# First-norm and indexer-key roots as a GpSimd power with one Newton step, and the first layer's indexer products with the low part last

## The chip, the cores and the metric

The kernel runs on one core of one Trainium2 chip. The metric is the device time of one execution in microseconds. The time given for a kernel is the median of several runs. A profile is one further execution, recorded by the hardware profiler.

The core has five engines, each with its own in-order instruction queue: PE (TensorE, matrix products; its weight loads are listed as PEld), DVE (VectorE), ACT (ScalarE), POOL (GpSimd) and SP (SyncE, which here only issues DMAs). [...]

## The reference

Two decoder layers on one sequence of 512 tokens of width 1024. What matters here is the beginning of the program and of each layer:

```python
x = layer_norm(x, ln_in_g, ln_in_b)                 # the first norm, over 1024 columns
for i in range(2):
    h = x @ w_in[i]                                 # columns partitioned: ..., qi (256), ki (32), wi (8)
    ki = rope(layer_norm(ki, idx_k_g, idx_k_b))     # the indexer key: a norm over 32 columns
    qi = rope(qi)
    # indexer: scores of qi with ki, weighted by wi, pick 128 keys for each query (top_k)
    # then sliding-window attention, sparse attention over the picked keys, output projection,
    # x = LN(alpha*x + mix); gated FFN and per-layer embedding; x = LN(...)
```

`layer_norm(x) = (x - mean) * rsqrt(var + 1e-5) * g + b`. Both changes concern the `rsqrt` of the first norm and of the indexer key's norm, and the product of the normed x with the 296 indexer columns (qi, ki, wi) in the first layer.

## The kernel before, in words

The 512 tokens are four blocks of 128 (`t` = 0 to 3). Every matrix product is made of three passes (`mm3`, lines 323 to 327): each operand is split into a high part (rounded to the fast float format) and a low part (the remainder), and the products high x high, high x low of the weight, and low of x x high are summed in one bank. x in transposed form lies in `fh` (high) and `fl` (low).

How a block gets from memory to its indexer product:

- **The norm** (`ln_in`, lines 386 to 400). Block 0 has its mean and variance from DVE. Blocks 1 to 3 have theirs from ACT (`ln_in_sums`, lines 380 to 384: a sum, a small multiply, and `squares` at line 377). DVE then subtracts the mean and multiplies with g in two halves (line 397), `rstd_of` (lines 352 to 365) makes the root, and line 400 multiplies with the root and adds b, again in two halves. Gains and biases are read from four banks filled by PE at the start (line 345).
- **The root**, `rstd_of(var, n)`: one DVE instruction for -0.5(var + eps) (line 357), one that makes a first guess by arithmetic on the bits (line 358), then three Newton steps of two DVE instructions for each of n columns (lines 363 and 364). That is 8 DVE instructions for n = 1 and 14 for n = 2.
- **To features** (`to_features`, lines 432 to 441): PE transposes the block in two groups of four (line 438), ACT copies each group to `fh` (line 440), DVE subtracts to get `fl` (line 441).
- **The indexer product** (`project`, lines 535 to 546, called from `start` at line 826): eight rows `k` of the weights, three matmuls of 296 columns each, 24 for a block, in the order high, weight-low, x-low for each `k`.
- **After it** (`gi_out`, lines 555 to 594): DVE takes mean and variance of the 32 key columns (lines 562 to 564); for each pair of blocks the key's root is made (line 578, n = 2: blocks 0 and 1 when block 1 is done, 2 and 3 when block 3 is done); `rope` (lines 502 to 517) multiplies with the rotary tables on DVE (line 511), adds on POOL (line 513), copies the high part (line 516) and subtracts the low part on POOL (line 517). PE's transposes of the results follow later (line 523), then the indexer's scores (lines 638 to 651: PE 645, ACT 647, DVE 648), then top-k on DVE (lines 659 and 660).

Beside this run the weights: SP loads them in pieces (line 240), ACT rounds the high part (line 278), POOL subtracts the low part (line 279); five split pieces fit (`W_AHEAD`). A piece's place is given back by `w_rel` when the last product with it has been written down; for the indexer weights that is in block 3. And the rotary tables (`rotary`, lines 453 to 491): products on ACT (line 473), 6 and then 4 additions of 128 x 192 on POOL (line 477), two sines on ACT, some copies.

What sets the order: the Python code writes the instructions down in an order in which streams (`start`, `index`, `rest`, `attention`, `topk`) are interleaved by estimated costs, and the planner of the tile framework then arranges each engine's queue from its own timing estimates, an earlier-written instruction first among those that it takes to be ready. On the chip each queue runs strictly in the order arranged. `tc.issue_after(ins)` adds one more rule: what is written inside it comes behind `ins` on the same engine. All of `gi_out(t)` for t < 3 of the first layer is put behind the norm of block t + 1 in this way (line 822).

## Time and profile before

| | |
|---|---|
| median of 3 runs | 1251.45 us (1251.43 to 1251.7) |
| the profiled execution's own time | 1251.81 us |
| its span (first to last recorded instruction) | 1249.7 us |
| PE busy | 1225.9 us, 98% |
| DVE, POOL, ACT busy | 765.2, 682.9, 576.4 us |
| POOL weight splits of line 279 | 148, 351.3 us |

A row of the timeline begins with the start in us from the beginning of the span and the duration in us; then come engine, line of the kernel, operation, what is written and read, the shape, and how many consecutive instructions are merged in the row. In square brackets stands how long the engine had been idle before, and whose end released it. A row of the windows gives, for a stretch of time, its length and then the busy time of PE, PEld, DVE, ACT and POOL. A row of the waits gives who waited for whom: us in total, how often, the longest.

### The profile page before, as it was taken

How to read it: one execution, taken by the hardware profiler on the slowest of the kernel's cores; microseconds unless marked ns; L12 is line 12 of the kernel's file. 1: busy time of each engine (PE TensorE's matmuls, PEld its weight loads, DVE VectorE, ACT ScalarE, POOL GpSimd, SP SyncE). 2: the span in 40 equal slices, each digit the busy share in tenths (PEclk: the TensorE clock that was granted, in tenths of full speed). 3: DMA queues.
4: the chain of work that ended last, by engine and by line, in shares of the span. 5: the costliest groups of instructions: out<-in, count | busy, mean ns of one | idle time of the engine just before them, and what ended most of it. 6: DMA issues, size and time to landing. Idle time of an engine off the chain costs nothing.

```text
span 1249.7 us, 18006 instructions
## 1 busy us (share of the span) xinstructions
PE 1225.9 (98%) x6552; PEld 1029.9 (82%) x6552; DVE 765.2 (61%) x1678; ACT 576.4 (46%) x1193; POOL 682.9 (55%) x555
## 2 busy tenths in 40 slices
PE   7999999999999999999999999999999999999996
PEld 5998777988888888888899987689888888888885
DVE  7699954682727272726677998286555555555365
ACT  6577763442434343433337787534343333333331
POOL 6885532566566666663169754234757575757400
PEclk9999999999999999999999999999999999999999
DMA  5232311333232323034033203114323333321321
GB/s 177 78 92 85 95 42 35 119 118 118 85 118 84 118 85 118 18 118 140 2 89 114 101 21 117 52 54 149 99 87 105 97 105 99 103 83 52 101 84 50
DMA packets 89264, 112.74 MB, mean 90 GB/s; under 512 B 5460, under 2 KB 66132, under 8 KB 89176
## 3 DMA queue, kind: packets, MB, share of 16 engines
q1 hardware_dynamic: 88504, 111.58, 28.5%
q8 instruction: 51, 0.84, 0.3%
q14 instruction: 37, 0.30, 0.1%
q10 hardware_dynamic: 672, 0.03, 0.0%
HBM read 109.49 MB, written 2.10 MB: 89 GB/s over the span
## 4 chain that ended last, share of the span: by engine, by line
PE 82%; POOL 5%; DVE 3%; issue 3%; ACT 3%; DMA 3%; SPq 0%; DVEq 0%; ACTq 0%; POOLq 0%
PE bank L325 24%; PE bank L326 24%; PE bank L327 24%; PE bank L715 3%; PE bank L684 3%; PE bank L721 2%; POOL wsp L279 2%; DMA wst<-in_w_pg_dram 2%; POOL wsp L257 1%; PE bank L523 1%; PE bank L438 1%; PE bank L732 1%; ACT wsp L278 1%; DVE slot L273 1%; POOL slot L517 1%
## 5 line engine op out<-in xcount | busy, mean ns | idle before, releaser
L279 POOL TENSOR_TENSOR wsp<-wst,wsp 128x1024 fp32r<-128x1024 f32 (+2 forms) x148 | 351.3, 2389 | 244.4 <-ACT wsp L278 240.8
L326 PE MATMUL bank<-fl,wsp 128*128 128x512 f32 (+1 forms) x768 | 284.8, 372 | 0.4 <-DVE fl L441 0.4
L325 PE MATMUL bank<-fh,wsp 128*128 128x512 f32 (+1 forms) x768 | 283.6, 372 | 1.0 <-ACT fh L440 1.0
L327 PE MATMUL bank<-fh,wsp 128*128 128x512 f32 (+1 forms) x768 | 283.1, 371 | 0.0
L278 ACT CAST wsp<-wst 128x1024 fp32r<-128x1024 f32 (+2 forms) x148 | 151.6, 1033 | 166.4 <-PE bank L327 126.2
L325 PE MATMUL bank<-wsp,fh 128*128 128x256 f32 (+3 forms) x512 | 165.2, 326 | 3.6 <-DVE work L648 2.0
L874 DVE TENSOR_TENSOR t2k<-bank,t2k 128x512 f32<-128x512 f32 x44 | 30.4, 692 | 222.0 <-PE bank L327 222.0
L326 PEld LDWEIGHTS bank<-fl,wsp 128*128 128x128 f32 x768 | 144.6, 188 | 25.7 <-DVE fl L441 0.9
L325 PEld LDWEIGHTS bank<-fh,wsp 128*128 128x128 f32 x768 | 143.6, 188 | 26.8 <-ACT fh L440 1.9
L327 PEld LDWEIGHTS bank<-fh,wsp 128*128 128x128 f32 x768 | 144.6, 188 | 24.9
L327 PE MATMUL bank<-wsp,fl 128*128 128x256 f32 (+3 forms) x512 | 163.7, 322 | 1.4 <-DVE fl L441 0.8
L326 PE MATMUL bank<-wsp,fh 128*128 128x256 f32 (+3 forms) x512 | 164.7, 322 | 0.0
L257 POOL TENSOR_TENSOR wsp<-slot,wsp 128x512 fp32r<-128x512 f32 x100 | 141.6, 1442 | 29.0 <-ACT wsp L256 29.0
L325 PE MATMUL bank<-wsp,slot 128*128 128x512 f32 x392 | 153.8, 392 | 0.0
L326 PE MATMUL bank<-wsp,slot 128*128 128x512 f32 x392 | 152.7, 390 | 0.0
L327 PE MATMUL bank<-wsp,slot 128*128 128x512 f32 x392 | 148.4, 390 | 0.0
L790 DVE TENSOR_TENSOR x<-bank,x 128x512 f32<-128x512 f32 x140 | 91.5, 684 | 88.5 <-PE bank L327 88.5
L904 ACT CAST slot<-t2k 128x256 fp32r<-128x256 f32 (+1 forms) x104 | 49.8, 497 | 144.1 <-DVE t2k L874 102.5
L257 POOL TENSOR_TENSOR wsp<-t2k,wsp 128x512 fp32r<-128x512 f32 x40 | 57.5, 1448 | 92.4 <-ACT wsp L256 92.4
L325 PEld LDWEIGHTS bank<-wsp,fh 128*128 128x128 f32 x512 | 97.6, 191 | 11.9 <-ACT fh L440 2.4
L327 PEld LDWEIGHTS bank<-wsp,fl 128*128 128x128 f32 x512 | 97.5, 191 | 7.9 <-DVE fl L441 1.1
L326 PEld LDWEIGHTS bank<-wsp,fh 128*128 128x128 f32 x512 | 98.0, 191 | 6.5 <-issue 1.2
(152 smaller groups left out, 2004.6 us busy)
## 6 DMA issues: line engine op xcount, KB each, us to landing
wst<-in_w_gu_dram SPq DMA_DIRECT2D x88, 512.0 KB, 3.5
slot<-in_w_down_dram SPq DMA_DIRECT2D x80, 256.0 KB, 2.8
wst<-in_w_in_dram SPq DMA_DIRECT2D x16, 512.0 KB, 3.6
wst<-in_w_o_dram SPq DMA_DIRECT2D x16, 512.0 KB, 3.8
wst<-in_w_pg_dram SPq DMA_DIRECT2D x16, 512.0 KB, 4.2
wst<-in_w_in_dram SPq DMA_DIRECT2D x8, 256.0 KB, 2.7
lng<-in_ln_g_dram SPq DMA_DIRECT2D x4, 512.0 KB, 4.8
lnb<-in_ln_b_dram SPq DMA_DIRECT2D x4, 512.0 KB, 5.5
```

Source lines behind the costliest of these rows:

```text
L257: G.tensor_tensor(w[:, 1, j], src[j], w[:, 0, j], OP.subtract)
L278: A.copy(w[:, 0, :a * n], st[:, :a * n])
L279: G.tensor_tensor(w[:, 1, :a * n], st[:, :a * n], w[:, 0, :a * n], OP.subtract)
L325: PE.matmul(o, sh, mh, start=start, stop=False, skip_group_check=again)
L326: PE.matmul(o, sh, ml, start=False, stop=False, skip_group_check=again)
L327: PE.matmul(o, sl, mh, start=False, stop=stop, skip_group_check=again)
L684: PE.matmul(ps[:, o:o + nn], qT[kind, t, g][:, j * 128:(j + 1) * 128], kT[c, s][:, k0:k0 + nn], start=(s == 0), stop=(s == 1))
L715: PE.matmul(o[u * 64:(u + 1) * 64], vt[b0 + b][:, c * 64:(c + 1) * 64], pts[b][:, u], start=b == 0, stop=b == nb - 1)
L721: PE.transpose(ps[:, j * 128:(j + 1) * 128], es[j][:, b * 128:(b + 1) * 128], idf)
L790: V.tensor_tensor(xt[t][:, c], ps, xt[t][:, c], OP.add)
L874: V.tensor_tensor(a, ps[1, f], a, OP.mult)
L904: A.copy(h[0], src)
```

## The change

Three edits. First, a new function `root_of` takes the place of `rstd_of` in `ln_in` (four uses, n = 1) and in the indexer key's norm of `gi_out` (two uses in each layer, n = 2). The other norms keep `rstd_of`. `root_of` has one DVE instruction for the variance plus eps, one POOL instruction (`tensor_tensor` with the operation `pow`, against a constant tile of -0.5), and three DVE instructions that make one Newton step. In the n = 1 form the first of these three overwrites what the power reads, so it has to come after it. Second, the first six of the ten additions on POOL for the rotary tables are put behind block 0's power. Third, in the first layer `project_fresh` writes the indexer product of a block with the 16 matmuls on the high part of x first and the 8 on the low part last; the places of the weight pieces are given back among the last eight matmuls of block 3.

```diff
+    half = small.tile([128, 2], F32, name="half", tag="half", bufs=1)
+    G.memset(half, -0.5)
+
+    def root_of(var, n=1, of=1):
+        v = sm(n, f"lnv{n}")
+        s = sm(n, f"lns{n}")
+        t = sm(n, f"lnt{n}")
+        V.tensor_scalar(v, var, of * EPS, 1.0 / of, op0=OP.add, op1=OP.mult)
+        last["root"] = G.tensor_tensor(s, v, half[:, :n], OP.pow).ins
+        if n == 1:
+            V.tensor_scalar(v, v, -0.5, None, op0=OP.mult)
+            V.tensor_scalar(t, s, s, v, op0=OP.mult, op1=OP.mult)
+            V.tensor_scalar(s, t, 1.5, s, op0=OP.add, op1=OP.mult)
+        else:
+            V.tensor_tensor(t, s, s, OP.mult)
+            V.scalar_tensor_tensor(t, t, -0.5, v, op0=OP.mult, op1=OP.mult)
+            V.scalar_tensor_tensor(s, t, 1.5, s, op0=OP.add, op1=OP.mult)
+        return s
...
-        rs = rstd_of(var, of=of)                    # in ln_in
+        rs = root_of(var, of=of)
...
-            for pr in products:                     # in rotary
-                G.tensor_tensor(ang[:, :n], pr, ang[:, :n], OP.add)
+            with tc.issue_after(last["root"]) if bits == 7 else nullcontext():
+                for pr in products:
+                    G.tensor_tensor(ang[:, :n], pr, ang[:, :n], OP.add)
...
+    def project_fresh(ws, n, t, done, rel):
+        parts = [(i, r, *from_f(t, k)) for k, (i, r) in
+                 enumerate((i, r) for i, w in enumerate(ws) for r in range(len(w[0])))]
+        o = acc()[:, :n]
+        for k, (i, r, sh, sl) in enumerate(parts):
+            PE.matmul(o, sh, ws[i][0][r], start=k == 0, stop=False)
+            PE.matmul(o, sh, ws[i][1][r], start=False, stop=False)
+            yield 2 * 0.218 * n / 512
+        for k, (i, r, sh, sl) in enumerate(parts):
+            PE.matmul(o, sl, ws[i][0][r], start=False, stop=k == len(parts) - 1)
+            if i < rel and r == len(ws[i][0]) - 1:
+                w_rel()
+            yield 0.218 * n / 512
+        done(t, o)
...
-                rs = rstd_of(mv[:, :, 1], 2)        # in gi_out
+                rs = root_of(mv[:, :, 1], 2)
...
-                yield from project(ws, 296, (t,), from_f, done, 3 * (t == 3))   # in start
+                if l == 0:
+                    yield from project_fresh(ws, 296, t, done, 3 * (t == 3))
+                else:
+                    yield from project(ws, 296, (t,), from_f, done, 3 * (t == 3))
```

## The prediction

> **What bounds the kernel now.** I read the page first, then the windows, then the waits of PE, then the timeline of the stretches where PE waits.

> ```profile
> span 1249.7 us, 18006 instructions
> ...
> 15.00:22.00 7.00, 6.23 (x26) 6.01 (x26) 6.14 (x20) 6.94 (x16) 6.83 (x7) 1.00 0.67 178
> 22.00:30.00 8.00, 6.93 (x49) 5.96 (x48) 8.00 (x30) 5.44 (x15) 4.12 (x10) 1.00 0.25 69
> 40.00:50.00 10.00, 9.54 (x64) 9.16 (x63) 8.17 (x26) 4.99 (x14) 10.00 (x16) 1.00 0.57 160
> 61.00:100.00 39.00, 39.00 (x327) 38.64 (x326) 37.01 (x107) 28.43 (x78) 31.02 (x37) 1.00 0.41 122
> ```

> ```profile
> PE bank L438 <- DVE x L400: 2.0, 1, 2.0
> PE bank L325 <- DVE work L648: 2.0, 2, 1.0
> ...
> PE bank L327 <- DVE fl L441: 0.8, 1, 0.8
> PE bank L327 <- DVE lns L358: 0.6, 1, 0.6
> ```

> From 61 us on PE has no hole in 39 us; a change that shortens DVE or POOL work there is worth nothing. The holes are at the start. From 15 to 22 us PE lacks 0.77 us and ACT is full (6.94 of 7); from 22 to 30 PE lacks 1.07 and DVE is full (8.00 of 8); from 40 to 50 POOL is full. So three engines bound the start in turn, and a microsecond won there stays won only if PE then finds work without a hole. The whole time of the profiled execution, 1251.81 us, is 2.1 more than its span; the median is 0.4 below it. I make the sum as a difference and take it from the median. What a measurement of this kernel can tell from no change is about 0.2%, 2.5 us; the waits above are 5.4 us in sum, so the stakes are small.

> **Block 0's root.**

> ```profile
> 6.63 0.87 POOL L463 TENSOR_SCALAR t2k<-t2k 128x192 f32<-128x192 f32 x1
> ...
> 8.74 0.15 DVE L357 TENSOR_SCALAR lnv<-bmv 128x1 f32<-128x1 f32 x1
> 8.80 0.74 DVE L397 SCALAR_TENSOR_TENSOR x<-x,bmv,bank 128x512 f32<-128x512 f32 x1
> ...
> 9.46 0.15 DVE L358 TENSOR_SCALAR lns<-lnv 128x1 int32<-128x1 int32 x1
> 9.64 0.27 DVE L363 TENSOR_SCALAR lnt<-lns,lnv 128x1 f32<-128x1 f32 x1
> ...
> 11.06 0.21 DVE L364 TENSOR_SCALAR lns<-lnt,lns 128x1 f32<-128x1 f32 x1
> ...
> 12.19 1.97 PE L438 MATMUL bank<-idf,x 128*128 128x128 f32 x8 [2.04 <-DVE x L400]
> ...
> 12.57 1.15 ACT L377 ACTIVATE t2k<-x,lnm 128x1024 bf16<-128x1024 f32 x1
> ...
> 13.72 1.05 ACT L440 CAST fh<-bank 128x512 fp32r<-128x512 f32 x2
> ```

> The power has no row. The lower bound is the smallest two-input POOL operation, the upper the dearest one on a small tile:

> ```profile
> L695 POOL TENSOR_TENSOR ek<-sink,ng 128x4 f32<-128x4 f32 x16 | 3.2, 202 | 12.4 <-DVE ng L688 12.4
> L463 POOL TENSOR_SCALAR t2k<-t2k 128x192 f32<-128x192 f32 x2 | 1.7, 862 | 0.2
> ```

> 0.20 to 0.86 us; I take 0.3, near the first, because one element per partition lies next to four and far from 192. POOL is free from 7.50 (the six additions now stand behind the power), so the power runs from about 8.95 to 9.25, beside the second half of L397 (to 9.54). Then three DVE operations (0.15, 0.27, 0.21 and gaps) end near 10.2, where L364 ended at 11.27: x of block 0 is 1.1 us earlier. But PE does not start on it: the first four transposes are done by half of L438's 1.97 us, about 13.2, and ACT copies them at 13.72, when its squares for block 1 have ended (12.57 + 1.15). In ACT's queue the squares stand ahead. So I count 0 for this root; if the planner now puts the copy ahead of the squares, up to 1.1. The cover is 0.5 + 1.1: up to a power of some 1.9 us (0.3 more than these 1.6) block 0 loses nothing either.

> **The low part last, block 0.**

> ```profile
> 13.12 3.47 POOL L279 TENSOR_TENSOR wsp<-wst,wsp 128x888 fp32r<-128x888 f32 x2
> ...
> 14.34 0.61 PE L325 MATMUL bank<-wsp,fh 128*128 128x296 f32 x1 [0.19 <-ACT fh L440]
> ...
> 14.75 0.45 PE L326 MATMUL bank<-wsp,fh 128*128 128x296 f32 x1
> ...
> 15.24 1.28 DVE L441 TENSOR_TENSOR fl<-bank,fh 128x512 fp32r<-128x512 f32 x2
> ...
> 15.97 0.61 PE L327 MATMUL bank<-wsp,fl 128*128 128x296 f32 x1 [0.77 <-DVE fl L441]
> ...
> 16.38 0.45 PE L325 MATMUL bank<-wsp,fh 128*128 128x296 f32 x1
> ...
> 16.63 0.45 PE L326 MATMUL bank<-wsp,fh 128*128 128x296 f32 x1
> ...
> 19.76 1.41 DVE L400 SCALAR_TENSOR_TENSOR x<-x,lns,bank 128x512 f32<-128x512 f32 x2
> ...
> 21.56 1.28 PE L438 MATMUL bank<-idf,x 128*128 128x128 f32 x8
> ```

> Running, matmuls follow each other by 0.25 us (16.38, 16.63); after a stop the first takes 0.41 (15.97 to 16.38). The third matmul comes at 15.97 instead of 15.00, and the restart costs 0.16: 1.13 us, which goes, since now 16 matmuls precede the first that needs `fl` (ready at 16.52). The next thing that could be late is the weights' low part: the eighth matmul (16.2) wants the second piece, the fourteenth (17.7) the third, and both are split by 16.59, the second about halfway. No new stop. Block 0 then ends at 21.56 - 1.13 = 20.4. Is x of block 1 there? Its L400 ended at 21.17. Its chain on DVE loses L358 (0.15) and two pairs of L363 and L364 (0.96) and gains one multiply (0.15): 0.96 less, 20.2. Its power waits in POOL's queue behind the splits to 16.59, but DVE has `fl` to make until 16.52, so the wait is covered; if the power came behind one more split (half of 3.47, 1.7 us), DVE, with the next block's L397, L400 and `fl` queued behind, would stand that long. Value: **-1.13 us**.

> **Block 1.**

> ```profile
> 20.97 1.11 ACT L473 ACTIVATE t2k<-t2k 128x192 f32<-128x192 f32 x4
> ...
> 23.32 0.30 PE L326 MATMUL bank<-wsp,fh 128*128 128x296 f32 x1
> ...
> 24.21 0.41 PE L327 MATMUL bank<-wsp,fl 128*128 128x296 f32 x1 [0.59 <-DVE lns L358]
> ...
> 24.45 0.30 PE L325 MATMUL bank<-wsp,fh 128*128 128x296 f32 x1
> 24.59 0.29 PE L326 MATMUL bank<-wsp,fh 128*128 128x296 f32 x1
> ```

> The wait is laid to L358, but what the matmul reads is `fl`, ahead of L358 in DVE's queue: 24.21 instead of 23.46 (pitch 0.14), with a restart 0.10 longer: **-0.85 us**. Behind 16 matmuls (2.2 us) `fl` is in time. One price is open: ACT's four products L473 (to 22.08) may stand ahead of the copy of block 1, which would now be wanted at 21.3; that would cost 0.8. They wait for POOL's additions, which the change pushes back, so I take them to come behind the copy: 0.

> **The clock.** A matmul of 296 columns took 0.45 us at 16.63 and 0.30 at 23.32: PE ran at about half rate in its first microseconds. Eight transposes took 1.28 at 21.56 and 1.03 in the next block, so the full rate came after 21.56: between 5.6 and 7.3 us behind the stop that ended at 15.97. With the same distance from 14.34, where PE now runs through, it comes up to 1.6 us earlier. Block 0 gets at most 0.2 from that, since x of block 1 is there at 20.2; the transposes get the difference of their two rows:

> ```profile
> 26.11 1.40 DVE L400 SCALAR_TENSOR_TENSOR x<-x,lns,bank 128x512 f32<-128x512 f32 x2
> ...
> 27.31 1.03 PE L438 MATMUL bank<-idf,x 128*128 128x128 f32 x8
> ```

> **-0.25 us**, bounds 0 and -0.45 (with the 0.2 of block 0). [...]

> **Blocks 2 and 3.** Block 1 would end at 27.31 - 2.2 = 25.1, but x of block 2, ready at 27.51, gains only two roots, 1.9 us, so 25.6: its second four transposes are wanted at 25.1 + 0.5, on the edge: **+0.25** for that meeting, bounds 0 and 0.5. Block 3's x has gained three roots (2.85) and is not late. The weights of these four blocks come free later (and with them SP's next loads, ACT's casts and POOL's splits), in the last third of block 3 instead of from its ninth matmul on; 10 matmuls by 0.14 us are 1.4, less than what the block itself is earlier. POOL, full from 40 to 50 us, takes on six powers (1.8 us) before that; it had gaps of that size in the 22 to 30 window (4.12 of 8 busy). I take 0, with 1 us to either side: L325 waits 1.0 for L648 once in each layer, and layer 0's hole may close or grow.

> **The key's root.** Each loses ten DVE instructions. In layer 0 it stands beside full PE. In layer 1:

> ```profile
> 652.51 1.25 DVE L357 TENSOR_SCALAR lnv<-kmv 128x2 f32<-128x2 f32 x1
> ...
> 656.34 0.91 DVE L580 SCALAR_TENSOR_TENSOR kin<-kin,lns,ikb 128x32 f32<-128x32 f32 x2
> ...
> 658.03 0.47 DVE L648 SCALAR_TENSOR_TENSOR work<-bank,wi,causal 128x256 f32<-128x256 f32 x1
> ```

> ```profile
> 654.39 2.40 POOL L279 TENSOR_TENSOR wsp<-wst,wsp 128x1024 fp32r<-128x1024 f32 x1
> ```

> L648 releases PE from layer 1's 1.0 us hole, and this root stands ahead of it in DVE's queue. If the power gets in before the split at 654.39, L580 starts near 655.1 and PE gains up to 1.0; if behind it (656.8), L580 starts at 657.7, and PE loses 1.35. The queue decides; I take **-0.25**, a little on the good side of the middle.

> Sum: -1.13 - 0.85 - 0.25 + 0.25 - 0.25 = -2.2 us. 1251.45 - 2.2 = **1249.2 us**.

> **The rivals.**

> *More comes through.* The planner puts the copy of block 0 ahead of the squares (1.1), or the layer 1 hole closes (0.75 more than counted), or layer 0's (1.0). For it: DVE, full from 22 to 30, loses 2.85 us there. With two of them: 1247.4 us.

> *Given back before 61 us.* PE arrives 2 us early at work fed by POOL, full from 40 to 50, and by DVE, 37.01 of 39 from 61 to 100. Against it: both chains start from PE's own blocks and move with them. 1251 us.

> *The power is dear.* This is the one that ends slower. A power P long stands between two DVE instructions with everything of DVE queued behind it. Block 0 hides 1.9, block 1 the splits' time, but blocks 2 and 3 lie where DVE is full: each loses P - 0.3. At P = 1.4 that eats the 2.2 us; from there it decides. At P = 3 it is 5.4 for these and 1.1 for block 0 less 2.2, so 1255.8. For it: POOL's price depends on the operation (L463's 862 ns on a tile of 192); against it: one element.

> *Only the first power is dear.* What it takes above 1.9 us delays block 0, all else as forecast; from 4.1 us on the kernel is slower than before. Against it: the first of the two L463 took 0.87 and the two together 1.7, so there the first use cost nothing. [...]

> *It doesn't do what it says.* The planner, which may move PE's other work between the halves, could leave PE as it was: 1251.4.

> **How the numbers follow.** Forecast 0.48, more 0.22, given back 0.12, dear 0.12, only the first dear 0.03, nothing 0.03. Faster by over 2.5 us: all of "more", and four tenths of the forecast's case, whose own range is 1247.9 to 1250.4: 0.42. Slower: nine tenths of "dear", half of "first" and a quarter of "given back" (a grown hole): 0.16. The rest, 0.42, is within. The range 1246.8 to 1252.6 leaves out most of "dear" and the end of "more".

> **What would show it.** In the profile after: no wait of L327 on `fl` in blocks 0 and 1; block 0's transposes at about 11.1, yet its first matmul still near 14.3; block 1's transposes near 20.4 instead of 21.56; a POOL row for the power with about 0.3 us; a shorter hole where L648 ends it near 658. I am wrong if the power's row is above 1.4 us, if DVE stands waiting for it behind a split, or if PE's holes between 40 and 61 grow by as much as the start gained.

## The result, and the profile after

The kernel after takes 1257.82 us (median of 6 runs, 1256.99 to 1260.49), the kernel before 1251.58 us in the same comparison (6 runs, 1251.23 to 1252.53). The ratio is 1.0053, interval 1.0042 to 1.0063: slower by 0.5%, 6.2 us, where 2.2 us less was forecast and 1252.6 was the end of the range.

The page of the kernel after: its span, its busy time of PE, and the clock that PE was granted in 40 slices.

```profile
span 1255.9 us, 17960 instructions
...
PE 1231.4 (98%) x6552; PEld 1034.5 (82%) x6552; DVE 755.6 (60%) x1622; ACT 577.7 (46%) x1193; POOL 687.4 (55%) x564
...
PEclk9899999999999999999999999999999999999998
```

The first thing to see is that PE is busy for 5.5 us *longer* (1225.9 before), with the same matmuls. Its idle time, span less busy, is 24.5 us against 23.8. So the loss of 6.2 us is not idle time in the main, it is PE working more slowly. The 8 in the second slice (31 to 63 us) says where: the granted clock falls there. The mean clock of this execution is 0.993, that of before 0.998.

Windows of the kernel after: one stretch of the prediction first, then the two stretches where time was lost and, inside each, the stretch at half clock (PEclk 0.50). Lines of the code are now 20 to 37 higher: L400 has become L420, L517 L538, L523 L544, L645 and L648 L682 and L685; the power is L361.

```profile
22.00:30.00 8.00, 7.98 (x57) 7.17 (x56) 7.97 (x25) 4.73 (x12) 7.12 (x13) 1.00 0.35 103
32.00:64.50 32.50, 30.25 (x182) 28.63 (x181) 18.19 (x46) 17.15 (x45) 28.64 (x40) 0.89 0.29 81
37.00:47.00 10.00, 8.12 (x50) 7.01 (x49) 6.22 (x11) 3.72 (x8) 10.00 (x12) 1.00 0.41 109
47.05:53.86 6.81, 6.50 (x23) 6.21 (x23) 4.08 (x11) 3.73 (x13) 6.18 (x14) 0.50 0.22 73
656.12:682.30 26.18, 22.83 (x152) 22.30 (x151) 14.14 (x40) 15.07 (x44) 21.93 (x26) 0.93 0.41 119
664.86:668.26 3.40, 3.40 (x13) 3.40 (x12) 1.71 (x5) 1.62 (x7) 3.11 (x7) 0.50 0.00 0
```

The same two stretches in the kernel before, cut so that they begin and end at the same count of matmuls:

```profile
35.00:62.40 27.40, 25.94 (x182) 25.35 (x181) 17.11 (x56) 17.24 (x46) 24.77 (x33) 1.00 0.32 88
653.40:676.20 22.80, 21.21 (x151) 20.69 (x151) 16.05 (x51) 14.79 (x45) 21.55 (x26) 1.00 0.49 137
```

The start was won: from 22 to 30 us PE has no hole any more (7.98 of 8, before 6.93), and the matmul at which the next stretch begins, the 121st, starts at 31.99 instead of 34.98. Then the next 182 matmuls take 32.50 us instead of 27.40, 5.1 us more: 0.8 of it idle time (2.25 against 1.46) and 4.3 busy time (30.25 against 25.94). In layer 1 the same count of matmuls (the windows list 152 and 151) takes 26.18 us instead of 22.80, 3.4 more: 1.8 idle (3.35 against 1.59) and 1.6 busy. The rest of the program differs by 0.7 us in all. -3.0 + 5.1 + 3.4 + 0.7 = 6.2.

Counts mix wide and narrow matmuls, so a second measure is used below, equal work: the time at which PE's matmuls have streamed as many columns as those of the kernel before at a given time, worked out from the matmul records of each profile. By it the kernel after is 2.4 us ahead where before stands at 35 us, 2.4 behind at 50, 2.1 behind at 61, 2.7 behind at 640 and 6.1 behind at 690. The lead of the start turns into a lag between 40 and 50 us, and layer 1 adds the rest.

The busy time is the clock. In layer 0 it is at half from 47.05 to 53.87, in layer 1 from 664.86 to 668.27. The timeline shows its price on one kind of matmul; PE of the kernel after, at half rate and just behind it:

```profile
51.09 0.52 PE L326 MATMUL bank<-wsp,fh 128*128 128x384 f32 x1
51.41 0.52 PE L327 MATMUL bank<-wsp,fl 128*128 128x384 f32 x1
...
54.28 0.34 PE L325 MATMUL bank<-wsp,fh 128*128 128x384 f32 x1
```

A matmul of 384 columns starts every 0.32 us instead of every 0.174 (mean pitch at full clock just behind it). An estimate from this pitch: the 6.50 us of work would have taken 3.0 less; in layer 1, 11 matmuls by 0.146 are 1.6, the whole of the busy surplus there. In layer 0 another 0.5 is only apparent: 14 of the 182 are of 384 columns where before has 296. 0.8 us of busy time in layer 0 is not assigned.

Where the idle time comes from, and what stands ahead of the fall of the clock, is in the waits. PE's waits in the kernel after:

```profile
PE bank L325 <- DVE work L685: 3.3, 1, 3.3
...
PE bank L458 <- DVE x L420: 1.3, 2, 1.1
PE bank L544 <- POOL slot L538: 1.3, 2, 1.1
```

Layer 0, the timeline of DVE and POOL, then of DVE and PE, between 37 and 48 us, kernel after:

```profile
37.98 1.14 DVE L360 TENSOR_SCALAR lnv<-kmv 128x2 f32<-128x2 f32 x1
...
39.40 1.83 POOL L279 TENSOR_TENSOR wsp<-wst,wsp 128x768 fp32r<-128x768 f32 x1
41.20 0.87 POOL L534 TENSOR_TENSOR t2k<-t2k 128x128 f32<-128x128 f32 x2
42.03 0.70 POOL L361 TENSOR_TENSOR lns<-lnv,half 128x2 f32<-128x2 f32 x1
...
43.12 2.36 POOL L279 TENSOR_TENSOR wsp<-wst,wsp 128x1024 fp32r<-128x1024 f32 x1
45.45 1.40 POOL L538 TENSOR_TENSOR slot<-t2k,slot 128x256 fp32r<-128x256 f32 x2
...
42.76 0.42 DVE L367 TENSOR_TENSOR lnt<-lns 128x2 f32<-128x2 f32 x1 [3.64 <-POOL lns L361]
43.21 2.30 DVE L368 SCALAR_TENSOR_TENSOR lnt<-lnt,lnv 128x2 f32<-128x2 f32 x1
...
46.22 0.54 PE L544 MATMUL bank<-idr,slot 128*128 128x128 f32 x4 [1.12 <-POOL slot L538]
```

POOL works without a gap (10.00 of 10 in the window from 37 to 47). PE, early, wants the transposes of the rotary results, and the low part that they read (L538 at 45.45) stands behind a weight split (L279, 43.12 to 45.48). With the smaller holes PE has 1.88 us idle from 37 to 47 (10.00 - 8.12). The clock drops at 47.05. The key's power stands in the same queue, behind splits and rotary work: DVE waits 3.64 us for an operation of 0.70.

POOL's rotary work also comes later in itself, although PE is early. Block 1's ten transposes, in the kernel before and in the kernel after:

```profile
40.84 0.96 PE L523 MATMUL bank<-idr,slot 128*128 128x128 f32 x10
43.21 1.05 PE L544 MATMUL bank<-idr,slot 128*128 128x128 f32 x10
```

PE had other work until then and did not stop here, but what it needed from POOL for them was done at 43.16 (the L538 that starts at 42.70, 0.46 long), behind two splits of 1.84 and 1.83 us.

Layer 1, timeline of the kernel after:

```profile
654.95 4.19 POOL L279 TENSOR_TENSOR wsp<-wst,wsp 128x768 fp32r<-128x768 f32 x2
659.10 0.87 POOL L534 TENSOR_TENSOR t2k<-t2k 128x128 f32<-128x128 f32 x2
659.93 0.70 POOL L361 TENSOR_TENSOR lns<-lnv,half 128x2 f32<-128x2 f32 x1
...
660.66 0.33 DVE L367 TENSOR_TENSOR lnt<-lns 128x2 f32<-128x2 f32 x1 [5.63 <-POOL lns L361]
...
663.57 0.44 PE L325 MATMUL bank<-wsp,fh 128*128 128x384 f32 x1 [3.31 <-DVE work L685]
```

Here the chain is direct: the power waits for two splits and two additions (654.95 to 659.93), DVE stands 5.63 us with L685 queued behind, and PE's hole before L325 is 3.31 us where it was 1.02. 1.3 us behind the hole's end, the clock is at half.

### The profile page after: what moved, and what is told of

Same layout as the page of the kernel before. It is cut to its first block, busy times and chain, and to the rows that moved or that the text cites. A ratio compares the mean times of both kernels' runs of the same rounds, so it can differ in the third digit from the quotient of the medians.

```text
span 1255.9 us, 17960 instructions
## 1 busy us (share of the span) xinstructions
PE 1231.4 (98%) x6552; PEld 1034.5 (82%) x6552; DVE 755.6 (60%) x1622; ACT 577.7 (46%) x1193; POOL 687.4 (55%) x564
## 4 chain that ended last, share of the span: by engine, by line
PE 87%; POOL 3%; DVE 3%; issue 2%; ACT 2%; DMA 2%; SPq 0%; DVEq 0%; POOLq 0%; ACTq 0%
PE bank L325 25%; PE bank L326 25%; PE bank L327 25%; PE bank L721 3%; PE bank L752 3%; PE bank L758 2%; POOL wsp L279 2%; DMA wst<-in_w_pg_dram 1%; PE bank L544 1%; DVE slot L273 1%; PE bank L458 1%; PE bank L682 1%; PE bank L769 1%; DMA wst<-in_w_in_dram 1%; DVE fl L461 0%
## 5 line engine op out<-in xcount | busy, mean ns | idle before, releaser
L279 POOL TENSOR_TENSOR wsp<-wst,wsp 128x1024 fp32r<-128x1024 f32 (+2 forms) x148 | 351.3, 2389 | 253.6 <-ACT wsp L278 252.9
L326 PE MATMUL bank<-fl,wsp 128*128 128x512 f32 (+1 forms) x768 | 284.9, 372 | 0.4 <-DVE fl L461 0.4
L325 PE MATMUL bank<-fh,wsp 128*128 128x512 f32 (+1 forms) x768 | 283.7, 372 | 1.0 <-ACT fh L460 1.0
L327 PE MATMUL bank<-fh,wsp 128*128 128x512 f32 (+1 forms) x768 | 283.1, 371 | 0.0
L325 PEld LDWEIGHTS bank<-fh,wsp 128*128 128x128 f32 x768 | 143.6, 188 | 26.8 <-ACT fh L460 1.9
L326 PEld LDWEIGHTS bank<-fl,wsp 128*128 128x128 f32 x768 | 144.7, 188 | 25.6 <-DVE fl L461 0.9
L327 PEld LDWEIGHTS bank<-fh,wsp 128*128 128x128 f32 x768 | 144.7, 188 | 25.0
L325 PE MATMUL bank<-wsp,fh 128*128 128x256 f32 (+3 forms) x480 | 155.7, 328 | 3.6 <-DVE work L685 3.3
L326 PE MATMUL bank<-wsp,fh 128*128 128x256 f32 (+3 forms) x480 | 155.5, 324 | 0.3 <-POOL wsp L279 0.3
L327 PE MATMUL bank<-wsp,fl 128*128 128x256 f32 (+3 forms) x480 | 155.1, 325 | 0.0
L325 PE MATMUL bank<-wsp,slot 128*128 128x512 f32 x392 | 153.8, 392 | 0.0
L326 PE MATMUL bank<-wsp,slot 128*128 128x512 f32 x392 | 152.8, 390 | 0.0
L327 PE MATMUL bank<-wsp,slot 128*128 128x512 f32 x392 | 148.3, 390 | 0.0
L325 PEld LDWEIGHTS bank<-wsp,fh 128*128 128x128 f32 x480 | 91.9, 192 | 10.7 <-DVE work L685 3.7
L327 PEld LDWEIGHTS bank<-wsp,fl 128*128 128x128 f32 x480 | 91.6, 191 | 7.9 <-issue 2.7
L326 PEld LDWEIGHTS bank<-wsp,fh 128*128 128x128 f32 x480 | 92.1, 192 | 6.4 <-POOL wsp L279 0.6
```

What stands on the lines that cost most here:

```text
L279: G.tensor_tensor(w[:, 1, :a * n], st[:, :a * n], w[:, 0, :a * n], OP.subtract)
L325: PE.matmul(o, sh, mh, start=start, stop=False, skip_group_check=again)
L326: PE.matmul(o, sh, ml, start=False, stop=False, skip_group_check=again)
L327: PE.matmul(o, sl, mh, start=False, stop=stop, skip_group_check=again)
```

## The experiments

Three theories at the beginning, as the expectations have them. A: the key's power waits behind weight splits in POOL's queue, DVE stands with the score products behind it, and PE runs dry; the rest of the change keeps its gain of about 2 us. B: the new order of the first layer, which gives the weights back late, starves PE from 44 to 48 us. C: a power costs too much wherever it stands. Differences below are of medians of one comparison, so before has a median of its own in each: 1251.75 in the first.

**The key's root as before, all else as after.**

```diff
-                rs = root_of(mv[:, :, 1], 2)        # in gi_out
+                rs = rstd_of(mv[:, :, 1], 2)
```

> The whole change but for the indexer key's root, which is made on DVE as before in both layers. Theory A (the key's power waits in POOL's queue behind weight splits, DVE stands with the indexer's score products behind it, PE runs dry and falls to half clock): 1249.5 us, the start's gain of about 2 us stays; no stretch of half clock after 25 us, layer 1's hole back at about 1.0. Rival B (the new order of the first layer, with the weights released late, is what starves PE from 44 to 48 us): 1253 to 1254, half clock near 47 still there. Rival C (a power costs too much wherever it stands): over 1251.6.

1255.38 us (1254.01 to 1256.43), ratio 1.0029 (1.0019 to 1.0039). In layer 1 the hole and the half clock are gone, in layer 0 they are not. Its timeline, and its window at half clock:

```profile
42.83 2.37 POOL L279 TENSOR_TENSOR wsp<-wst,wsp 128x1024 fp32r<-128x1024 f32 x1
45.15 0.46 POOL L538 TENSOR_TENSOR slot<-t2k,slot 128x128 fp32r<-128x128 f32 x1
...
45.66 1.05 PE L544 MATMUL bank<-idr,slot 128*128 128x128 f32 x10 [1.93 <-POOL slot L538]
```

```profile
47.10:53.90 6.80, 6.52 (x26) 6.24 (x27) 2.95 (x7) 3.62 (x11) 5.34 (x11) 0.50 0.18 62
```

A larger hole (1.93 us instead of 1.12), behind the same kind of split, without any power near it. A falls for layer 0 and stands for layer 1. The half clock near 47 us is what B expected, the time is above its 1253 to 1254.

**The key's root alone as power**, on the kernel before.

```diff
-                rs = rstd_of(mv[:, :, 1], 2)        # in gi_out, kernel before
+                rs = root_of(mv[:, :, 1], 2)
```

> The kernel before with nothing changed but the indexer key's root, as a power on POOL in both layers. Theory A: slower, 1256 to 1260, with a wait of DVE for the power of some 3 us in layer 0 and 5 us in layer 1, and half clock after at least one of them. Rival B: only layer 1's part, about 1255. If both are wrong: 1251.

1258.51 us (1258.34 to 1259.19), ratio 1.0055 (1.0041 to 1.0069), worse than the whole change. DVE's waits in it:

```profile
DVE lnt L367 <- POOL lns L361: 12.0, 2, 6.3
```

Two waits, 12 us of DVE standing; PE has a hole of 3.32 us before 664.2 and half clock from 664.83 to 668.24, and in layer 0 half clock from 50.43 to 53.84. The time lies in A's range (1256 to 1260). B expected about 1255.

**The first norm's root alone** (with the six additions behind it), and **the low part last alone**, each on the kernel before.

```diff
-        rs = rstd_of(var, of=of)                    # first_norm_alone, in ln_in
+        rs = root_of(var, of=of)
...
-                yield from project(ws, 296, (t,), from_f, done, 3 * (t == 3))   # low_last_alone
+                yield from (project_fresh(ws, 296, t, done, 3 * (t == 3)) if l == 0 else
+                            project(ws, 296, (t,), from_f, done, 3 * (t == 3)))
```

> The kernel before with only the first norm's four roots as powers, and the six additions behind the first. Theory A and B: 1250 to 1251, block 0's first matmul about 1 us earlier and then again a stop for the low part. Rival C: over 1252.5.

> The kernel before with only the first layer's indexer products reordered, low part last. Theory A: 1249.5 to 1250.5, the two stops for the low part gone. Rival B: over 1252.5, with holes of PE from 44 to 48 us.

First norm alone: 1254.35 us (1252.97 to 1255.06), ratio 1.0018 (1.0009 to 1.0027). Low part last alone: 1256.4 us (1255.45 to 1256.61), ratio 1.0036 (1.0023 to 1.0048). Neither is the gain that the forecast gave it. In the first, PE is early, meets x of block 1 late (a hole of 2.19 us before 20.2) and falls back to half clock from 22.36 to 29.19. In the second, windows of the stretch before the clock falls and behind it:

```profile
44.60:48.00 3.40, 1.68 (x17) 1.40 (x16) 0.96 (x2) 2.55 (x6) 3.40 (x9) 1.00 0.57 154
48.10:51.40 3.30, 3.30 (x15) 3.30 (x15) 1.51 (x5) 2.43 (x9) 3.30 (x7) 0.50 0.02 5
```

POOL full (3.40 of 3.40), PE idle for half of the stretch, and then half clock, with no power in the kernel at all. The three parts cost 6.8, 2.6 and 4.7 us alone and 6.2 together: they don't add up, and the planner arranges every queue anew each time. By equal work, the low part last alone is 0.6 us ahead of the kernel before at 35 us and 2.1 behind at 50; the key's root alone is 0.5 ahead and 3.6 behind. Both lose at POOL. The first norm alone loses elsewhere: it is already 1.6 us behind at 35 us, before POOL is full, and 1.8 at 50.

None of the three theories holds whole. B fits the low part last alone (over 1252.5, with a hole of 1.38 us before 47.88), but the key's root alone has such a hole too (1.31 us before 47.44), with the old order. A and B both expected a gain from the first norm alone (1250 to 1251). C expected over 1252.5 there, and over 1252.5 it is, but the four powers of the first norm took only 0.57 us each, and the low part last loses 4.7 us without any power. What the kernel after, `key_as_before` and the other two have in common is that PE waits for POOL's rotary results between 43 and 48 us (1.1 to 1.9 us). The next runs test that, under new letters. D: the half clock behind PE's holes is what makes these kernels slower; the holes only give back the start's gain. E: the half clock is only a mark of the hole and costs nothing by itself. F: POOL, with splits of 1.84 us among the rotary work, is what PE waits for from 38 to 50 us.

**POOL late without the change.** The kernel before, with three copies on POOL written ahead of block 2's rotary work in layer 0 (1.8 us in all; they ran at 33.4, 37.96 and 46.27). Their result is not used.

```diff
+                if l == 0 and t == 2:               # in gi_out, kernel before
+                    spare = t2k()
+                    for _ in range(3):
+                        G.tensor_copy(spare, causal)
```

> The kernel before with three unused POOL copies of 128 x 512 (about 2.2 us in sum) written ahead of block 2's rotary work in layer 0, nothing of the change. Theory D: PE's hole near 46 us grows by some 2 us, half rate follows for 3.4 or 6.8 us, 1255 to 1257. Rival E: the hole alone, about 1253.7. If POOL's delay is hidden: 1251.7.

1255.2 us (1252.75 to 1256.09, 11 runs; before 1252.23), ratio 1.002 (1.0011 to 1.0029). The profiled execution was the fastest of the 11. Its timeline, and its window of that time:

```profile
46.27 0.60 POOL L575 COPY t2k<-causal 128x512 f32<-128x512 f32 x1
46.84 0.45 POOL L517 TENSOR_TENSOR slot<-t2k,slot 128x128 fp32r<-128x128 f32 x1
...
47.34 1.05 PE L523 MATMUL bank<-idr,slot 128*128 128x128 f32 x10 [2.14 <-POOL slot L517]
```

```profile
43.40:46.80 3.40, 1.80 (x10) 1.48 (x9) 2.91 (x3) 0.00 (x0) 3.40 (x4) 1.00 0.69 171
```

Here is a hole like that of `key_as_before` (2.14 us) with nothing of the change in the kernel, so POOL's lateness suffices for it. By equal work this execution is 0.3 us ahead of the kernel before at 35 us and 2.4 behind at 50. In this execution the clock did *not* fall, and the hole alone cost about 1 us (1252.75 against 1251.81 for the profiled execution of before). The other ten runs of the same program, with mean clocks of 0.994 to 0.997, took 1253.17 to 1256.09. Part of the price is thus decided anew in each execution. A stretch at half clock may be that part, as D has it (1255 to 1257 was its range), but these ten have no trace, and the mean clock does not order them: three of the four with 0.997 took 1255.20 to 1255.39, the three with 0.994 took 1254.80 to 1256.09.

**Extra matmuls to fill the hole** (the key's root as before, eight extra products written ahead of block 2's transposes), **and the transposes written later** (two constants that say how much estimated PE time to let pass before the rotary transposes).

```diff
+                if l == 0 and t == 2:               # key_as_before_warm
+                    warm = bank("tp", 2)
+                    for _ in range(8):
+                        PE.matmul(warm, idr, fh[:, 0, :], start=True, stop=True)
...
-D_GI, D_KI, D_K, D_Q, AHEAD = 9.0, 13.0, 8.0, 10.0, 2    # key_as_before_d14, after_d14
+D_GI, D_KI, D_K, D_Q, AHEAD = 14.0, 17.0, 8.0, 10.0, 2
```

> The run key_as_before with eight extra matmuls of 512 columns (about 1.7 us at full rate, their result unused) on PE just ahead of block 2's transposes of layer 0, where that run has its hole of 1.9 us at 44 us. Theory D (what makes all these kernels slower is that PE's holes near 44 to 50 us drop it to half rate for one or two stretches of 3.4 us; the hole itself only gives back what the start gained): the hole is filled, no half rate after 25 us, 1255.4 - 3.4 = about 1252. Rival E (the half rate is only a mark of the hole and costs nothing by itself): the same 1255.4 or up to 1.7 more.

> The run key_as_before with the turns of the indexer's blocks written down later (D_GI 14 and D_KI 17 in place of 9 and 13), so that 17 to 27 of the next products stand ahead of block 2's transposes. Theory D: the hole at 44 us closes with useful work, full rate stays, 1250 to 1251. If the loss lies in the order elsewhere: over 1253.

> The whole change with the same later turns. Theory D: layer 0 mends, layer 1 keeps its hole of 3.3 us behind the key's power and its half rate: about 1254, with half rate only after 660 us. If the key's power alone makes the layer 0 hole: half rate near 47 stays, about 1257.

All three missed as tests of D. The extra matmuls came out behind the hole and not in it (1254.23 us, ratio 1.0016, 1.0007 to 1.0025): the hole stands ahead of block 1's transposes, I had written them ahead of block 2's. That the clock alone costs what I say it costs was therefore not tried on its own. Writing the transposes later (1257.33 us with either root, ratios 1.0043, 1.0031 to 1.0056, and 1.004, 1.0027 to 1.0052) moved the waits instead of closing them. With the key's root as before, the hole for POOL's results stayed (1.93 us before 47.75), and new ones came at 61 to 64 us with half clock from 63.78 to 70.61. In the whole change the hole for POOL went, and PE waited for copies on ACT instead (1.39 us before 50.16, 1.75 before 662.96). That profiled execution never lost the clock between 17 and 1246 us, and still took 1255.34, 3.1 more than the median of before: a loss of this size needs no half clock.

**Relieving POOL.** If F holds, taking work off POOL where PE meets it must take the loss away, and perhaps bring the gain of the start through. The low part of a few weight pieces is made on DVE: two pieces in each layer, or three. Which pieces was chosen from POOL's queue ahead of the two holes.

```diff
-            G.tensor_tensor(w[:, 1, :a * n], ...)                       # line 279
+            (V if i in (5, 6, 124, 125) else G).tensor_tensor(...)      # ..._dve
+            (V if i in (5, 6, 7, 124, 125, 126) else G).tensor_tensor(...)   # ..._dve3
```

> The run key_as_before with the low part of two weight pieces in each layer (those that come free at block 3, 128 x 768 each) made on DVE instead of POOL. Theory F (the start's gain of 2 to 3 us is lost because POOL, with these splits of 1.84 us each among the rotary work, is what PE waits for from 38 to 50 us): the hole at 44 us goes, full rate stays, 1249.5 to 1251. If POOL's queue is not it: 1255.

> The whole change with the same two pieces of each layer on DVE. Theory F, and for the key's power theory A (it waits behind splits on POOL): layer 0's hole goes, DVE's wait for the power in layer 1 falls from 5.6 us to what one 128 x 1024 split takes, 1250 to 1253. If the power is dear by itself: 1257.

> Control: the kernel before with two pieces of each layer on DVE and nothing of the change. POOL is relieved, but PE arrives as late as before: 1250.5 to 1251.5. If this alone is as fast as key_as_before_dve, the change's own gain is still lost.

> The whole change with three pieces of each layer on DVE, the third of 128 x 1024. Theory A: no split is left ahead of the key's power, DVE waits under 1.5 us for it, 1249 to 1251; a price may come from the third split on DVE (over 1 us) ahead of the indexer's work.

> after_dve3 with the key's root on DVE as before. If the key's power, once nothing stands ahead of it, is worth something: about 1 us over after_dve3, 1249.5 to 1250. If the power still costs: under 1248.5.

> Control to after_dve3: the kernel before with the same three pieces of each layer on DVE, nothing of the change. If the change itself is worth its 2 us once POOL's splits are out of the way: 1250.5 to 1251.5, some 2 us over after_dve3. If after_dve3 owes everything to the third piece: 1248.7, the same.

| low parts made on DVE | kernel before | after, key's root as before | after |
|---|---|---|---|
| none | 1251.75 | 1255.38, 1.0029 (1.0019 to 1.0039) | 1257.82, 1.0053 (1.0042 to 1.0063) |
| two in each layer | 1250.93, 0.9994 (0.9985 to 1.0003) | 1250.95, 0.9994 (0.9985 to 1.0002) | 1250.90, 0.9992 (0.9983 to 1.0001) |
| three in each layer | 1250.92, 0.9994 (0.9985 to 1.0003) | 1248.75, 0.9978 (0.997 to 0.9987) | 1248.68, 0.9973 (0.9964 to 0.9982) |

The medians of the first row are of different comparisons, and so is the last one of the third; the ratios are each against before in its own. The loss is gone in both rows of relief, as F expected. In the second row nothing of the gain is left against the control (1250.95 and 1250.90 against 1250.93). In the third row both kernels are 2.2 us faster than the control (1248.75 and 1248.68 against 1250.92), and the key's power neither gains nor loses.

It is tempting to read the 2.2 us as the forecast come through. The traces do not bear that out. Time against the kernel before at equal work, in us, minus for ahead; from the two marked rows 0.9 us is taken off, since in these two profiled executions the first block's transposes came 0.9 later than in others of the same start:

| | at 35 | 50 | 61 | 640 | 690 |
|---|---|---|---|---|---|
| after, none moved | -2.4 | 2.4 | 2.1 | 2.7 | 6.1 |
| before, two | -0.5 | -0.8 | -1.7 | -1.3 | -1.3 |
| key's root as before, two | -1.3 | -0.6 | -0.8 | 0.4 | 0.4 |
| after, two | -2.4 | -1.1 | -1.6 | -1.1 | -2.0 |
| before, three (marked) | -0.2 | -0.8 | -1.7 | 0.0 | -0.5 |
| key's root as before, three (marked) | -1.2 | -1.1 | -1.7 | -1.2 | -2.6 |
| after, three | -1.1 | -1.0 | -1.6 | -1.6 | -2.6 |

At 61 us the relieved kernel before is as far ahead as the relieved kernels after, or further. The start's lead of 1.1 to 2.4 us at 35 us is given back by then in every profile, with POOL relieved too. Relief brings the kernel after 3.7 us by 61 us (from 2.1 behind to 1.6 ahead) and the kernel before 1.7: it removes the loss, and the start stays worth nothing. Where the 2.2 us between the medians of the third row arise is not shown. Up to 0.9 lies between 640 and 690 us, in a layer that the first norm's root and the low part last do not touch; from 61 to 640 us single executions differ by more than 1 us.

The kernel after with three pieces on DVE beats both kernels. Its windows of layer 0, its wait of DVE in layer 1, and the timeline there:

```profile
40.00:50.00 10.00, 9.46 (x64) 9.09 (x63) 8.06 (x21) 4.46 (x13) 9.29 (x18) 1.00 0.53 159
47.05:53.86 6.81, 6.81 (x47) 6.78 (x47) 3.05 (x9) 4.52 (x16) 5.48 (x12) 1.00 0.01 2
```

```profile
649.31 0.95 DVE L279 TENSOR_TENSOR wsp<-wst,wsp 128x768 fp32r<-128x768 f32 x1
650.32 1.23 DVE L279 TENSOR_TENSOR wsp<-wst,wsp 128x1024 fp32r<-128x1024 f32 x1
...
653.03 0.70 POOL L361 TENSOR_TENSOR lns<-lnv,half 128x2 f32<-128x2 f32 x1
...
653.76 0.33 DVE L367 TENSOR_TENSOR lnt<-lns 128x2 f32<-128x2 f32 x1 [1.08 <-POOL lns L361]
```

Between 47.05 and 53.86, where the kernel after made 23 matmuls at half clock, there are now 47 at the full one. This execution lost the clock earlier instead, from 22.38 to 25.80, behind a wait of 1.65 us for x of block 1. DVE waits 1.08 us for the same power instead of 5.63. A low part costs DVE 0.95 and 1.23 us where POOL took 1.84 and 2.36. One reservation: moving the pieces also made the planner arrange all queues anew, so a run of this table is not one removed cost alone; the control in the first column shows how far that goes on the kernel before in its median, 1 us or less.

## Why the prediction was wrong, step by step

**Block 0's root: right in place, taken at the wrong end.** The timeline of the kernel after:

```profile
8.97 0.58 POOL L361 TENSOR_TENSOR lns<-lnv,half 128x1 f32<-128x1 f32 x1 [1.42 <-DVE lnv L360]
...
11.20 1.97 PE L458 MATMUL bank<-idf,x 128*128 128x128 f32 x8 [1.06 <-DVE x L420]
12.50 0.56 ACT L460 CAST fh<-bank 128x512 fp32r<-128x512 f32 x1
12.97 1.15 ACT L397 ACTIVATE t2k<-x,lnm 128x1024 bf16<-128x1024 f32 x1
13.12 0.62 PE L562 MATMUL bank<-wsp,fh 128*128 128x296 f32 x1
...
15.46 0.62 PE L563 MATMUL bank<-wsp,fh 128*128 128x296 f32 x1 [0.24 <-POOL wsp L279]
...
20.20 1.38 PE L458 MATMUL bank<-idf,x 128*128 128x128 f32 x8 [0.24 <-DVE x L420]
21.63 0.41 PE L562 MATMUL bank<-wsp,fh 128*128 128x296 f32 x1
```

The transposes come at 11.20 (forecast 11.1). The planner did put the copy ahead of the squares (12.50 before 12.97), so the first matmul comes at 13.12, not 14.3: the 1.1 us that the prediction kept for a rival, "More comes through".

**The power's price: mis-sized, not the cause.** The two forms in the kernel after:

```profile
L361 POOL TENSOR_TENSOR lns<-lnv,half 128x2 f32<-128x2 f32 x4 | 2.8, 703 | 0.0
L361 POOL TENSOR_TENSOR lns<-lnv,half 128x1 f32<-128x1 f32 x4 | 2.3, 573 | 1.4 <-DVE lnv L360 1.4
```

0.57 and 0.70 us where 0.3 was taken, inside the bounds of 0.20 and 0.86 (the six powers of layer 0 take 3.7 us of POOL, not 1.8), and far below the 1.4 at which the rival "dear" begins. That rival came nearest to the time (1255.8) for a reason that did not occur.

**The low part last, blocks 0 and 1: the stops went as said, the times came right by luck.** No stop on `fl` is left in block 0. "No new stop" was wrong: the second piece's low part is late at 15.46, with 0.24 us of idle time. Block 1's transposes start at 20.20 (forecast 20.4) and its first matmul at 21.63 instead of 23.08. But the 1.36 us by which the transposes are early (21.56 before) are not the 1.13 of the low part last. The first matmul is 1.22 earlier, where the prediction counted 0, and the block itself is only 0.14 shorter, because x of block 1 is now the last to arrive. Nor is x ready at 20.2, as the prediction had it: its L420 runs from 19.39 to 20.80, 0.37 us earlier than before and not 0.96, and PE starts at 20.20 on its first half.

**The start as a whole: right in this execution.** The 121st matmul comes 3.0 us earlier by count. Half a microsecond of that is the mix of widths, so about 2.5, where the terms of the start (-1.13, -0.85, -0.25, +0.25) make 2.0. Ten profiles hold the first norm's powers, and in six of them the clock falls back between 21.7 and 22.9 us, after PE has waited 1.5 to 2.2 us for x of block 1. With the low part last as well, 1.1 to 1.3 us of lead is left of 2.4 in those executions. The prediction had no term for this either.

**POOL from 40 to 50 us: the step that failed.** The prediction wrote "POOL, full from 40 to 50 us, takes on six powers (1.8 us) before that; it had gaps of that size in the 22 to 30 window" and "I take 0, with 1 us to either side". The gap of 22 to 30 us is indeed filled (7.12 of 8 against 4.12), but the question was not whether POOL can do six powers. It was whether PE, 2.4 us early, finds POOL's work done when it gets there. POOL did not deliver earlier for it: block 1's transposes come at 43.21 instead of 40.84, block 2's at 46.22 instead of 46.60. In place of the 0 of this term the runs showed a swing of 4.8 us, from 2.4 ahead at 35 us to 2.4 behind at 50, made of holes and of the half clock behind them. The prediction had this as the rival *Given back before 61 us* and argued it away ("both chains start from PE's own blocks and move with them"): the rotary chain does start from PE's blocks, but the splits between its operations start from DMA and ACT. The rival's case is what happened, and even with POOL relieved nothing of the start's lead was left at 61 us.

**The clock: treated only as a price of the start.** The prediction counted how much earlier the first full clock comes (a gain of 0.25 us) and never asked what a later hole does to it: that price stood at nothing in the sum. By the estimate from the pitch it is the larger part of the loss: about 3.0 us in layer 0 and 1.6 in layer 1, against 0.8 and 1.8 us of more idle time. It is why the rival's 1251 us was too small as well: a hole was priced at its length. The reading of the clock at the start was off too. The clock records have the full clock from 22.05 us in the kernel before, 6.1 us behind the stop that ended at 15.97, inside the 5.6 to 7.3 that the prediction read; but it comes directly behind a stretch of 3.41 us (18.64 to 22.05) in which PE never stops, while in the one before that PE is idle for 0.75 us. In the kernel after it comes at 19.74, again directly behind 3.41 us without a stop (16.32 to 19.74), and 4.3 us behind the stop that ended at 15.46: 2.3 us earlier than before and not at most 1.6. "The same distance" was the author's estimate, and the two kernels do not show it.

**The key's root: the bad end named, then half dismissed.** "If behind it (656.8), L580 starts at 657.7, and PE loses 1.35": this assumed one split ahead of the power. Two splits and two additions stood there (to 659.93), the hole grew by 2.3 us, and the clock took 1.6 more. The prediction took a value "a little on the good side of the middle", for an operation entering a busy queue. In place of -0.25 the runs showed +3.4 us in layer 1. One of the prediction's own signs of being wrong came true here: DVE stood waiting for the power behind splits, 3.64 and 5.63 us.

What is shown: the holes and their releasers; the half clock and its pitch; that POOL's lateness alone makes a hole like that of layer 0; that relief of POOL takes the loss of layer 0 away; that the key's power makes the loss of layer 1. What is argued: the 3.0 us for the clock in layer 0 comes from the pitch of one kind of matmul, and no run was built that takes the half clock away and leaves the hole. Why the low part last alone also loses the clock near 672 us, in a layer that it does not touch, stays open, and so does where the 2.2 us of the third row arise; all queues differ there.

## What to carry to other kernels

Before counting time won at the start, look for the next place where the engine that is now early meets a full one: here PE waited there, and the gain was gone (2.4 us ahead at 35 us, 2.4 behind at 50). Relieving the full engine took the loss away here, but it served the kernel without the change as well, so the control has to be relieved too before a gain is counted. An operation moved to a busy in-order queue costs what is queued ahead of it (3.6 and 5.6 us here), not its own 0.7 us. And a hole of PE should be priced twice, with its length and with the slower clock that may follow (here half the clock for 6.83 and 3.41 us).
